# A conformer-style layer on one core: who issues the transfers of the token mixer

## The chip, the cores and the metric

The kernel runs on one core of a Trainium2 chip. A core has TensorE (PE, matrix products into PSUM), VectorE (DVE), ScalarE (ACT), GpSimd (POOL) and SyncE (SP), each with its own queue of instructions that it takes in order, and 16 DMA engines that move data between DRAM and the on-chip SBUF. A transfer is an instruction in the queue of the engine that issues it. The metric is the device time of one execution in microseconds (us); less is better.

## The reference: what is computed

One trunk layer over 1152 tokens (128 of context, 1024 latents) of width 1024:

```python
x = x + HALF_STEP * m[2] * rms_norm(swiglu(h, p['ffn1_w13'], p['ffn1_w2']), gn[1])
h = modulate(rms_norm(x, gn[2]), m[3], m[4])
out, s_fin = token_mixer(h, s0, p, latent)
x = x + m[5] * rms_norm(out, gn[3])
h = modulate(rms_norm(x, gn[4]), m[6], m[7])
x = x + HALF_STEP * m[8] * rms_norm(swiglu(h, p['ffn2_w13'], p['ffn2_w2']), gn[5])
```

The token mixer is what the change touches. It projects h by w_in into r, k, v, g (512 wide each), the three inputs of a short convolution, and two gates of 1024. An RWKV-7 scan runs over r, k, v in both directions, 8 heads of 64:

```python
sa = jnp.einsum('bhij,bhj->bhi', S, -kk_t)
S = (S * w_t[:, :, None, :] + sa[..., None] * (kk_t * a_t)[:, :, None, :]
     + v_t[..., None] * k_t[:, :, None, :])
return S, jnp.einsum('bhij,bhj->bhi', S, r_t)
```

Its outputs are normalised by head, get a bonus (the sum of r k r_k over a head, times v), are gated by sigmoid(g) and projected; the convolution's branch is projected too; the two are merged by the sigmoid gates and projected by w_out.

## The kernel before

Activations lie by channels: tiles of 128 channels by 384 tokens (TW), the tokens in three thirds. Every dense product is made of three products of split operands (lo*hi, hi*lo, hi*hi). `load_w` brings weights in pieces of 128x4x128 (256 KB) into `wst`, of which there are three buffers; ACT makes the high half `whi` (L138), another engine the low half `wlo` (L139), in the mixer POOL.

The mixer lies between the two FFNs and mixes two kinds of work. **Dense products** come from `proj`: 1056 blocks of three matmuls `pj` (L705 to L707) of 128x384; after eight blocks a PSUM bank is full and is evacuated by a function that `proj` is given:

- `to_dram` (L716, L717): ACT copies or passes it through a function into `fso`, and the tile is stored to DRAM: r into rows of `opd`, v into `vd`, the gates into `gd`, `gad`, `gbd`.
- `k_to_dram` (L729, L730): the same for k, stored by `mirrored`, a pattern whose outer dimension is the two heads of a pair (2x64x384).
- `ev_cb` (L797 to L799): POOL multiplies by the convolution, and the tile goes to `cbvd`.

**The scan** has 18 items, a group of heads and a part of the tokens of both directions each. Its operands go through DRAM, since they come by channels and are wanted in other orders. `stage_k` loads r, k and factors (`or` L945, `ok` L890, `od` L892, `oi` L893, v L900), makes kk (stored at L922) and the bonus (ACT L907, stored into `bvd` at L908). `stage_v` loads v (`lv`) and turns it on PE (`vt`). `stage_b`, once for each direction of an item, loads 768 KB of operands (`ops`, L957, one buffer), takes decays (L961 to L982), makes products `scr` (L988), masks them into `e` (ACT L990, POOL L991), and copies the small blocks N out (`nt_`, ACT L995), which L996 stores to `nd`. `solve` loads them back (`un`), inverts them on VectorE (L1036, L1037) with a second trip through DRAM (`xdd`, `tb`), and `step` (L1112 on) does the scan's chunks with `sq`, `yp` and the state tiles `zv`.

A scheduler orders each engine's instructions by priorities and by data. The scan is traced at a high one (`chain()`, `beside()`), `fill(GI)` deals 40 dense blocks after each item, further jobs come in three lanes beside them, and weight loads are moved ahead by `lead`. All DMAs of the mixer stand in SP's queue. PE's order is fixed by the program, so where a scan product is late, the dense blocks behind it wait too.

Of the kernel before, what the change touches and what calls it, by code (L numbers as in the profile page):

```python
# [16 lines left out]
PSUM = bass.MemoryType.PSUM  # L17
DRAM = bass.MemoryType.DRAM
# [8 lines left out]
TW = T // NT  # L27
# [33 lines left out]
def body(ctx: ExitStack, tc: tile.TileContext, I: dict, y_prompt, y_sample, new_state):  # L61
# [16 lines left out]
    def pd(name="pd"):  # L78
        """a PSUM bank for a dense product, in the phases without the scan"""
        rr[0] += 1  # L80
        tag = ("mm", "sq", "yy", "mm", "sq", "oc")[rr[0] % 6]
        return psp.tile([128, TW], F32, name=name, tag=tag, bufs=1 if tag in ("yy", "oc") else 2)
# [5 lines left out]
    # ---------------------------------------------------------------- constants  # L88
# [27 lines left out]
    # ---------------------------------------------------------------- DRAM scratch  # L116
    xd = [[dram.tile([128, TW], F32, name=f"xd{k}_{t}") for t in range(NT)] for k in range(8)]
    # per two pairs: of direction 0 decay and the factors of kk and k, r, kk and k (each the other way round for the
    # second head of a pair), of direction 1 the factors and decay
# [16 lines left out]
    # ---------------------------------------------------------------- pieces  # L136
# [6 lines left out]
    def load_w(src, nk, eng=V):  # L143
        out = []
        with tc.high_priority(offset=lead[0]):
            for k0 in range(0, nk, 4):
                n = min(4, nk - k0)
                st = wp["st"].tile([128, 4, 128], F32, name="wst", tag="wst")
                hi = wp["hi"].tile([128, 4, 128], F32R, name="whi", tag="whi")
                lo = wp["lo"].tile([128, 4, 128], F32R, name="wlo", tag="wlo")  # L150
                SP.dma_start(st[:, :n], src[k0 * 128:(k0 + n) * 128].rearrange("(k p) m -> p k m", p=128))
                split(hi[:, :n], lo[:, :n], st[:, :n], eng)
                out += [(hi[:, k], lo[:, k]) for k in range(n)]
        return out
# [4 lines left out]
    class Beside:  # L159
        """small products, issued after the dense products traced so far"""  # L160
# [14 lines left out]
    class Later:  # L175
        """work beside the dense products, each piece of it so many of them after the one before"""
# [98 lines left out]
    def postnorm(t, O, ssum, gp, spill, want_sum, xpool, sp):  # L275
        """x += gate * rms(O), in place of O; with want_sum the scale of the next norm."""
        G1, G2, G3, GO = GAPS[t == 2 and len(GAPS) > 1]
        xo = []
        for k in range(8):
            x = xpool(k, t)  # L280
            SP.dma_start(x, xd[k][t])
            xo.append(x)
        yield G1
        rs = compact(ssum, 3, ones, 1, 1.0 / D, 1e-6, PE=PB)
        yield G2
        bc = bcast(rs, sp, PB)
        for k in range(8):
            if GO and k:
                yield GO
            a = tmp("poa")  # L290
            for lo, hi, c in SEGS[t]:
                V.scalar_tensor_tensor(out=a[:, lo:hi], in0=O[k][t][:, lo:hi], scalar=gp[:, k, c:c + 1], in1=bc[:, lo:hi], op0=ALU.mult, op1=ALU.mult)
            (V if want_sum or k % 2 else G).tensor_tensor(out=O[k][t], in0=a, in1=xo[k], op=ALU.add)
            if spill:
                SP.dma_start(xd[k][t], O[k][t])
            if want_sum:
                sq_acc(ssum, O[k][t], k == 0, eng=V if k > 5 else G)
        if want_sum:
            yield G3
            rs = compact(ssum, 3, ones, 1, 1.0 / D, 1e-6, PE=PB)  # L300
            yield G2
            return bcast(rs, sp, PB)

    # modulation columns
    def mod_first(mp, h):
        """half of the channels of the first shift and scale, the scale in part on the vector engine"""
# [72 lines left out]
    # ---------------------------------------------------------------- FFN  # L379
# [68 lines left out]
    # ================================================================ FFN 1  # L448
    with ExitStack() as ph:
# [4 lines left out]
        def x_third(t, xp, PE, gap):  # L454
            """a third of the tokens by channels, and the scale of its norm"""
# [123 lines left out]
    # ================================================================ token mixer  # L579
# [3 lines left out]
    # ================================================================ FFN 2  # L583
    with ExitStack() as ph:
# [7 lines left out]
        def rows_of(name, tag, src, k, eng):  # L592
            """a channel block of the last third by tokens"""
            ps = psp.tile([128, 3, 128], F32, name="pfl", tag="sc")
            for i in range(3):
                PB.transpose(ps[:, i], src[:, i * 128:(i + 1) * 128], ident)
            dst = hp.tile([128, 3, 128], F32, name=name, tag=f"{tag}{k}_0")
            if eng is S:
                S.activation(out=dst, in_=ps, func=AF.Copy)
            else:  # L600
                V.tensor_copy(dst, ps)
            return dst
# [50 lines left out]
def mixer(nc, tc, pool, env):  # L653
# [14 lines left out]
    # derived per-channel parameters  # L668
# [9 lines left out]
    # per half of the partitions: the factors of b~ and k~ in the order of its rows  # L678
# [19 lines left out]
    # ------------------------------------------------------------ dense fillers  # L698
    def proj(col, evac, ts=range(NT)):
        """a projection, one block of its rows at a time"""  # L700
        w = load_w(w_in[:, col:col + 128], 8, G)
        for t in ts:
            ps = e.psp.tile([128, TW], F32, name="pj", tag="mm")
            for k, ((hi, lo), (xh, xl)) in enumerate(zip(w, hx(t))):
                PE.matmul(ps, lo, xh, start=(k == 0), stop=False)  # L705
                PE.matmul(ps, hi, xl, start=False, stop=False)  # L706
                ins = PE.matmul(ps, hi, xh, start=False, stop=(k == 7))  # L707
                if k < 7:
                    yield ins
            evac(t, ps)  # L710
            yield ins

    def to_dram(dst, func=AF.Copy, **kw):
        def f(t, ps):
            o = e.tmp("fso", tag="s")
            S.activation(out=o, in_=ps, func=func, **kw)  # L716
            SP.dma_start(dst[:, t * TW:(t + 1) * TW], o)  # L717
        return f

    def mirrored(p, row, sign, t0, n):  # L720
        """a row of the operands of a pair, and for the second head the row after or before it"""
# [4 lines left out]
    def k_to_dram(p):  # L726
        def f(t, ps):
            o = e.tmp("fso", tag="s")
            S.activation(out=o, in_=ps, func=AF.Copy)  # L729
            SP.dma_start(mirrored(p, 5, -1, t * TW, TW), o)  # L730
# [15 lines left out]
    with ExitStack() as ph:  # L746
# [26 lines left out]
        def job_conv(j):  # L773
# [21 lines left out]
            def ev_cb(t, ps):  # L795
# [3 lines left out]
                SP.dma_start(cbvd[j][:, t * TW:(t + 1) * TW], o)  # L799
# [68 lines left out]
        def shifted(t, d):  # L868
            """(column, source token, count) of the tokens of a third that have a neighbour."""
# [12 lines left out]
        # ------------------------------------------------------------ per pair, per block of tokens  # L882
        def stage_k(p, t0, n, bon=True):
            """kk and the bonus, of a pair of heads and a block of tokens"""
# [17 lines left out]
            def bonus():  # L902
# [5 lines left out]
                SP.dma_start(bvd[p][:, t0:t0 + n], o)  # L908
# [18 lines left out]
        def stage_v(p, t0, n, zv):  # L927
            """V by tokens, of a pair of heads and a block of tokens"""
# [19 lines left out]
        def zi(g, b):  # L948
            """the place of V and of the outputs of a quarter of the latents"""
            return b if g == 0 else (1, 0, 3, 2)[b]  # L950

        def stage_b(g, d, t0, A, it):
            """operands of a direction for the two chunks of tokens t0.., of two pairs of heads"""
# [42 lines left out]
            SP.dma_start(diag(nd[it], d, s0, nb), N)  # L996
# [11 lines left out]
        def diag(t_, d, s0, nb):  # L1008
            """the blocks of a direction, partition by partition of the rows of a chunk"""
            return bass.AP(tensor=t_.tensor, offset=t_.offset + (d * 16 + s0 * 4) * 1024, ap=[[32, 128], [4096, nb], [1, 32]])  # L1010

        def every4(t_, r, n):
            """the partitions 4 v + r of a tile, first n columns"""
# [3 lines left out]
        def solve(A, it):  # L1017
            """(I - N)^-1 of the 32 diagonal 32x32 blocks of an item.

            Partition 4 v + rep has block v: the inverses of its four 8x8 diagonal blocks, and  # L1020
            of the whole the columns 8 b + 2 rep + cc, which follow from them row block by row block."""
# [69 lines left out]
        def group(products):  # L1091
            """products issued in a row, the first of which has the operand that comes last"""
# [8 lines left out]
        def cells(w, s):  # L1101
            """the states of two pairs in the operands of a chunk, head by head"""
# [9 lines left out]
        def step(A, chains, first):  # L1112
            """one chunk of two pairs of heads in each direction: (chunk of the item, its operands w[:, s], decay,
            outputs, next state). State and V are in w[:, s], a block of columns for each head: the state on
            the head's own half of the partitions, V on the other."""
# [185 lines left out]
        # the jobs that become possible after an item's scan  # L1301
# [3 lines left out]
        class Lane:  # L1305
            """jobs beside the scan: one at a time, a piece of it every so many blocks of dense products"""
# [28 lines left out]
        def fill(n):  # L1335
            """blocks of dense products, and the products beside the scan that are due"""
# [55 lines left out]
    # ================================================================ merge, output projection  # L1392
# [82 lines left out]
```

## Time and profile before

| | |
|---|---|
| median of 3 runs | 3303.96 us (3299.4 to 3308.2) |
| profiled execution, span | 3303.1 us; no other time is given for it |
| PE / PE weight loads busy | 3036.7 / 2850.3 us |
| VectorE / ACT / POOL busy | 1914.0 / 1201.1 / 395.3 us |
| mixer, roughly | 909 to 2215 us of the span |
| DMA | 347.25 MB, mean 105 GB/s |

The span is that of one execution under the hardware profiler. Instructions that issue a DMA don't count as busy. A piece "SPq" of the chain is time in which the chain's transfer was being issued in SP's queue, and "DMA" its time from then on until it landed.

### The profile page before, as it was taken

The page shows a single profiled execution, that of the slowest core. Times are in us where ns is not written, and L with a number is a line of the kernel's source. Part 1 is how long each engine was busy: PE and PEld are TensorE (multiplying, and loading weights), DVE is VectorE, ACT ScalarE, POOL GpSimd, SP SyncE. Part 2 cuts the span into 40 slices and gives each one's busy share as a digit, 9 for nine tenths or more (in the row PEclk, how much of TensorE's full clock was granted, in tenths as well). Part 3 has the DMA queues.
Part 4 walks back from the last instruction along what each step waited for, and adds up shares of the span by engine and source line. Part 5 has one row for each costly group of instructions (what it writes and reads, how often), then busy time and mean ns, then how long its engine had stood idle before and what let it go on. Part 6 is the DMA issues. An engine that isn't in the chain of part 4 may idle for free.

```text
span 3303.1 us, 54285 instructions
## 1 busy us (share of the span) xinstructions
PE 3036.7 (92%) x20956; PEld 2850.3 (86%) x20956; DVE 1914.0 (58%) x4282; ACT 1201.1 (36%) x2726; POOL 395.3 (12%) x327
## 2 busy tenths in 40 slices
PE   8999999999989677788888889899989999999998
PEld 5999999999978566677767777779989999999998
DVE  7535665556962244577877778856683233323356
ACT  5521111114546133355535456432454211121244
POOL 1000000001240111122323122100120000000012
PEclk9999999999999788799988899999999999999999
DMA  8423333225445242323333333345632111111244
GB/s 268 144 63 94 96 110 90 83 78 164 151 116 190 80 121 72 111 84 106 99 88 102 108 106 105 103 124 155 190 109 87 38 45 40 45 40 41 83 144 131
DMA packets 521742, 347.25 MB, mean 105 GB/s; under 512 B 76096, under 2 KB 497292, under 8 KB 521484
## 3 DMA queue, kind: packets, MB, share of 16 engines
q1 hardware_dynamic: 520856, 343.31, 35.2%
q8 instruction: 164, 2.69, 0.3%
q14 instruction: 94, 0.77, 0.1%
q10 hardware_dynamic: 308, 0.44, 0.0%
q0 software_dynamic: 320, 0.04, 0.0%
HBM read 277.37 MB, written 66.32 MB: 104 GB/s over the span
## 4 chain that ended last, share of the span: by engine, by line
PE 67%; DVE 16%; DMA 10%; ACT 3%; issue 2%; SPq 1%; POOL 0%; DVEq 0%; ACTq 0%; POOLq 0%
PE po L211 6%; PE po L210 6%; PE po L212 6%; PE pg L211 5%; PE pg L212 5%; PE pg L210 5%; PE pu L211 5%; PE pu L210 5%; PE pu L212 5%; PE pj L705 3%; PE pj L707 3%; PE pj L706 3%; DMA ops<-opd 3%; DMA oi<-opd 2%; DVE un L1036 1%
## 5 line engine op out<-in xcount | busy, mean ns | idle before, releaser
L138 ACT ACTIVATE whi<-wst 128x512 fp32r<-128x512 f32 (+1 forms) x578 | 353.1, 612 | 792.7 <-PE po L212 389.4
L139 DVE TENSOR_TENSOR wlo<-wst,whi 128x512 fp32r<-128x512 f32 (+1 forms) x480 | 325.2, 678 | 305.8 <-ACT whi L138 296.2
L705 PE MATMUL pj<-hh,wlo 128*128 128x384 f32 x1056 | 393.8, 373 | 4.3 <-ACT xcs L783 1.8
L706 PE MATMUL pj<-hl,whi 128*128 128x384 f32 x1056 | 393.7, 373 | 2.3 <-DVE hl L265 1.3
L707 PE MATMUL pj<-hh,whi 128*128 128x384 f32 x1056 | 391.9, 371 | 0.0
L211 PE MATMUL pg<-hl,whi 128*128 128x384 f32 x1056 | 355.9, 337 | 6.4 <-POOL hl L263 5.0
L210 PE MATMUL po<-ah,wlo 128*128 128x384 f32 x1056 | 355.4, 337 | 3.0 <-ACT ah L138 3.0
L210 PE MATMUL pg<-hh,wlo 128*128 128x384 f32 x1056 | 356.8, 338 | 1.4 <-DVE wlo L139 1.3
L211 PE MATMUL po<-al,whi 128*128 128x384 f32 x1056 | 354.8, 336 | 0.4 <-DVE al L139 0.4
L212 PE MATMUL pg<-hh,whi 128*128 128x384 f32 x1056 | 355.0, 336 | 0.0
L210 PE MATMUL pu<-hh,wlo 128*128 128x384 f32 x1056 | 355.0, 336 | 0.0
L212 PE MATMUL po<-ah,whi 128*128 128x384 f32 x1056 | 354.2, 336 | 0.0
L211 PE MATMUL pu<-hl,whi 128*128 128x384 f32 x1056 | 353.8, 335 | 0.0
L212 PE MATMUL pu<-hh,whi 128*128 128x384 f32 x1056 | 353.5, 335 | 0.0
L273 POOL TENSOR_TENSOR ss<-ss,sqt 128x384 f32<-128x384 f32 x78 | 88.5, 1138 | 1679.5 <-ACT sqt L272 1675.0
L426 DVE TENSOR_TENSOR sil<-sil,pu 128x384 f32<-128x384 f32 x132 | 72.8, 552 | 353.0 <-PE pu L212 353.0
L398 DVE TENSOR_TENSOR o<-o,po 128x384 f32<-128x384 f32 x288 | 159.2, 553 | 168.2 <-PE po L212 167.5
L705 PEld LDWEIGHTS pj<-hh,wlo 128*128 128x128 f32 x1056 | 215.6, 204 | 13.8 <-issue 2.1
L706 PEld LDWEIGHTS pj<-hl,whi 128*128 128x128 f32 x1056 | 215.9, 204 | 10.8 <-DVE hl L265 2.2
L707 PEld LDWEIGHTS pj<-hh,whi 128*128 128x128 f32 x1056 | 215.7, 204 | 7.0
L139 POOL TENSOR_TENSOR wlo<-wst,whi 128x512 fp32r<-128x512 f32 x98 | 134.6, 1376 | 622.7 <-ACT whi L138 486.1
L211 PEld LDWEIGHTS pg<-hl,whi 128*128 128x128 f32 x1056 | 199.7, 189 | 8.8 <-POOL hl L263 6.5
(621 smaller groups left out, 5848.6 us busy)
## 6 DMA issues: line engine op xcount, KB each, us to landing
wst<-in_ffn_w SPq DMA_DIRECT2D x324, 256.0 KB
wmod<-in_w_mod SPq DMA_DIRECT2D x144, 256.0 KB
ops<-opd SPq DMA_DIRECT2D x36, 768.0 KB
wst<-in_w_in SPq DMA_DIRECT2D x94, 256.0 KB
wst<-in_ffn_w SPq DMA_DIRECT2D x96, 192.0 KB
xo<-xd SPq DMA_DIRECT2D x64, 192.0 KB
wst<-in_w_out SPq DMA_DIRECT2D x48, 256.0 KB
opd<-zv SPq DMA_DIRECT2D x24, 384.0 KB
```

Source lines behind the costliest of these rows:

```text
L138: S.activation(out=hi, in_=src, func=AF.Copy)
L139: eng.tensor_tensor(out=lo, in0=src, in1=hi.bitcast(F32), op=ALU.subtract)
L210: PE.matmul(ps, lo, xh, start=(k == 0), stop=False)
L211: PE.matmul(ps, hi, xl, start=False, stop=False)
L212: later.tick(PE.matmul(ps, hi, xh, start=False, stop=(k == nk - 1)))
L273: eng.tensor_tensor(out=ssum, in0=ssum, in1=q, op=ALU.add)
L398: V.tensor_tensor(out=O[m][t], in0=O[m][t], in1=ps, op=ALU.add)
L426: V.tensor_tensor(out=s, in0=s, in1=pu, op=ALU.mult)
L705: PE.matmul(ps, lo, xh, start=(k == 0), stop=False)
L706: PE.matmul(ps, hi, xl, start=False, stop=False)
L707: ins = PE.matmul(ps, hi, xh, start=False, stop=(k == 7))
L1036: V.tensor_tensor(out=pv, in0=a, in1=b, op=ALU.mult)
```

## The change

The weight loads of `proj` are issued by POOL, the engine that makes `wlo` out of them. The stores of `to_dram`, `k_to_dram`, the bonus and N are issued by ACT, which makes these tiles, and the store of `ev_cb` by POOL, which makes that one. Sizes, patterns and buffers stay. The rest of the diff takes comments and docstrings out and leaves line numbers as they were.

```diff
-    def load_w(src, nk, eng=V):
+    def load_w(src, nk, eng=V, queue=SP):
...
-                SP.dma_start(st[:, :n], src[k0 * 128:(k0 + n) * 128].rearrange("(k p) m -> p k m", p=128))
+                queue.dma_start(st[:, :n], src[k0 * 128:(k0 + n) * 128].rearrange("(k p) m -> p k m", p=128))
...
     def proj(col, evac, ts=range(NT)):
-        w = load_w(w_in[:, col:col + 128], 8, G)
+        w = load_w(w_in[:, col:col + 128], 8, G, G)
...
             S.activation(out=o, in_=ps, func=func, **kw)
-            SP.dma_start(dst[:, t * TW:(t + 1) * TW], o)
+            S.dma_start(dst[:, t * TW:(t + 1) * TW], o)
...
             S.activation(out=o, in_=ps, func=AF.Copy)
-            SP.dma_start(mirrored(p, 5, -1, t * TW, TW), o)
+            S.dma_start(mirrored(p, 5, -1, t * TW, TW), o)
...
                 G.tensor_tensor(out=o, in0=o, in1=u_[t], op=ALU.mult)
-                SP.dma_start(cbvd[j][:, t * TW:(t + 1) * TW], o)
+                G.dma_start(cbvd[j][:, t * TW:(t + 1) * TW], o)
...
                 S.activation(out=o, in_=o, func=AF.Identity, bias=gb4[:, p:p + 1])
-                SP.dma_start(bvd[p][:, t0:t0 + n], o)
+                S.dma_start(bvd[p][:, t0:t0 + n], o)
...
-            SP.dma_start(diag(nd[it], d, s0, nb), N)
+            S.dma_start(diag(nd[it], d, s0, nb), N)
```

In the program this moves 94 weight loads (L151) and 12 stores (L799) to POOL, and 152 stores (84 at L717, 12 at L730, 20 at L908, 36 at L996) to ACT. The scheduler places everything anew.

SP's queue early in the mixer, while the first operands of the scan are loaded; the rows that stood there before and don't any more have a minus:

```order
 L922 DMA opd_110<-oi 2x64x256
 L890 DMA ok<-opd_110 128x1x256
 L892 DMA od<-opd_110 128x1x256
-L151 DMA wst<-in_w_in 128x4x128
 L957 DMA ops<-opd_110 128x12x128
 L893 DMA oi<-opd_110 128x1x256
-L730 DMA opd_110<-fso 2x64x384
-L717 DMA vd_113<-fso 128x384
 L900 DMA or<-vd_113 128x256
```

Ahead of the operand load L957 the weight load is gone, and ahead of the load of v (L900) the two stores.

ACT's queue in the same part of the program, from the decays of the first item to the store of its first N, before the change. In brackets stands what an instruction waits for: the work of an engine, or (DMAHW, DMASW) one of the counters that finished transfers raise, of which the transfers issued by SP and ACT share eight:

```order
L716 ACTIVATE fso<-pj 128x384 [waits PE_49]
L138 ACTIVATE whi<-wst 128x512 [waits DMAHW0_49,PE_49,Pool_49]
L907 ACTIVATE or<-or,gb_9063 128x256 [waits DVE_49]
L990 ACTIVATE e_10899<-scr 64x4x128 [waits DVE_49]
L995 ACTIVATE nt__10933<-ab_10895 32x128 x2
L990 ACTIVATE e_10899<-scr 64x4x128 [waits DVE_49]
L995 ACTIVATE nt__10933<-ab_10895 32x128 x2
L1000 ACTIVATE ab_10895<-bkt 128x512 [waits PE_49]
```

And in the changed program:

```order
L907 ACTIVATE or<-or,gb_9063 128x256 [waits DVE_49]
L138 ACTIVATE whi<-wst 128x512 [waits DMASW6_49,PE_49,Pool_49]
L908 DMA bvd_117<-or 128x256 [waits Activation_49]
L716 ACTIVATE fso<-pj 128x384
L717 DMA vd_113<-fso 128x384 [waits DMAHW0_49,Activation_49]
L990 ACTIVATE e_10899<-scr 64x4x128 [waits DVE_49]
L995 ACTIVATE nt__10933<-ab_10895 32x128 x2
L990 ACTIVATE e_10899<-scr 64x4x128 [waits DVE_49]
L995 ACTIVATE nt__10933<-ab_10895 32x128 x2
L1000 ACTIVATE ab_10895<-bkt 128x512 [waits PE_49]
L996 DMA nd_9071<-nt__10933 128x4x32 [waits DMAHW2_49,Activation_49]
```

Three stores now stand between the copies, each waits for the copy that makes its tile ("Activation"), and two of them for a counter besides.

POOL's queue around the masks of the first item in the changed program; before, the same rows stood there without the L151:

```order
+L991 TENSOR_TENSOR e_10899<-e_10899,cst 64x4x128 x2
+L139 TENSOR_TENSOR wlo<-wst,whi 128x512
+L151 DMA wst<-in_w_in 128x4x128
+L139 TENSOR_TENSOR wlo<-wst,whi 128x512
+L151 DMA wst<-in_w_in 128x4x128
+L139 TENSOR_TENSOR wlo<-wst,whi 128x512
+L151 DMA wst<-in_w_in 128x4x128
+L991 TENSOR_TENSOR e_10900<-e_10900,cst 64x4x128 x2
```

Each weight load follows the instruction that frees its buffer, in the same queue.

## Rows read from the trace of the kernel before

**Rows 1.** The page's busy times of each engine, and the share of each in the chain of work that ended last.

```profile
PE 3036.7 (92%) x20956; PEld 2850.3 (86%) x20956; DVE 1914.0 (58%) x4282; ACT 1201.1 (36%) x2726; POOL 395.3 (12%) x327
...
PE 67%; DVE 16%; DMA 10%; ACT 3%; issue 2%; SPq 1%; POOL 0%; DVEq 0%; ACTq 0%; POOLq 0%
```

**Rows 2.** Busy time by stretch of the span, for three parts of the mixer: start and end, length, each engine's busy us with its instructions, the granted TensorE clock, the busy share of the DMA engines, GB/s.

```profile
909.00:1060.00 151.00, 133.69 (x702) 124.73 (x700) 75.17 (x134) 80.23 (x150) 36.99 (x31) 0.94 0.45 145
1060.00:1340.00 280.00, 199.31 (x1454) 177.11 (x1453) 114.18 (x298) 86.35 (x217) 39.24 (x30) 0.79 0.35 103
1340.00:2215.00 875.00, 762.77 (x7686) 646.60 (x7685) 661.56 (x1828) 420.59 (x1140) 192.82 (x145) 0.92 0.35 99
```

**Rows 3.** The chain of work that ended last, pieces of it in order of time between 1060 and 1340 us: start, length, what.

```profile
1073.78 7.54 DMA opd<-fso
...
1097.42 3.97 SPq L151
...
1107.48 1.51 SPq L730
1109.10 9.07 DMA vd<-fso
1118.19 2.14 DMA or<-vd
...
1132.62 3.38 SPq L717
1136.11 9.09 DMA oi<-opd
...
1156.68 3.20 SPq L908
...
1249.74 10.69 DMA bvd<-or
...
1295.61 0.65 SPq L908
...
1318.62 1.42 SPq L908
```

**Rows 4.** SP's queue in order of time just after 1100 us: start, length of the issuing instruction, line, transfer.

```profile
1101.44 1.34 SPq L957 DMA_DIRECT2D ops<-opd  x1
1102.83 4.56 SPq L893 DMA_DIRECT2D oi<-opd  x1
```

**Rows 5.** The timeline of ACT and of PE at the same place: start, length, instruction, and in brackets how long the engine had been idle and what ended it.

```profile
1111.02 0.42 ACT L961 ACTIVATE sg<-ops 128x256 f32<-128x256 f32 x1 [11.05 <-DMA ops<-opd]
1116.77 3.48 PE L988 MATMUL scr<-e,bk 64*128 64x128 f32 x16 [10.09 <-DVE bk L978]
1123.96 0.60 ACT L1000 ACTIVATE ab<-bkt 128x512 f32<-128x512 f32 x1
```

**Rows 6.** What SP's queue waited for: us in total, times, longest. The first row is for the whole mixer (909 to 2215 us), the others for 1060 to 1340.

```profile
SPq L717 <- ACT fso L716: 75.2, 28, 10.7
...
SPq L151 <- POOL wlo L139: 32.0, 12, 10.3
...
SPq L996 <- ACT nt__11901 L995: 14.0, 1, 14.0
SPq L717 <- ACT fso L716: 9.8, 5, 4.2
```

**Rows 7.** The chain again, at 1593 us.

```profile
1593.21 2.90 DMA wst<-in_w_in
```

**Rows 8.** Durations of the issuing instructions in SP's queue by line (ns, least/median/most, first and last start in us). L996 has a row for each of its tiles; the first of its 36 is shown.

```profile
L717 SPq DMA_DIRECT2D gad<-fso x24: 319/326/1068, 1820.3 to 2200.3; - x24
L717 SPq DMA_DIRECT2D gbd<-fso x23: 319/332/506, 1854.8 to 2209.9; - x23
L717 SPq DMA_DIRECT2D opd<-fso x12: 319/439/3987, 918.7 to 1244.0; - x12
L717 SPq DMA_DIRECT2D vd<-fso x12: 319/440/2076, 946.7 to 1327.9; - x12
L717 SPq DMA_DIRECT2D gd<-fso x12: 319/434/860, 1332.7 to 1542.1; - x12
...
L730 SPq DMA_DIRECT2D opd<-fso x12: 492/516/1512, 931.7 to 1284.5; - x12
...
L908 SPq DMA_DIRECT2D bvd<-or x20: 315/358/4068, 1054.1 to 2003.5; - x20
...
L996 SPq DMA_DIRECT2D nd<-nt__10933 x1: 371/371/371, 1123.9 to 1123.9; - x1
```

**Rows 9.** Issues by ACT and by POOL at the start of the program: of ACT's four the longest and the shortest (start, length), of POOL's ten one of 4 rows and the one of 32 (ns, least/median/most).

```profile
0.74 0.59 ACTq L509 DMA_DIRECT2D rows<-in_c_ctx  x1
1.37 0.33 ACTq L512 DMA_DIRECT2D rows<-in_norm_g  x1
...
L528 POOL DMA_DIRECT2D rows<-in_k_k x1: 518/518/518, 2.5 to 2.5; - x1
...
L528 POOL DMA_DIRECT2D rows<-in_mu_shift x1: 535/535/535, 6.1 to 6.1; - x1
```

**Rows 10.** The dense products L705 over the whole program: count and mean (ns) of one matmul, and of PE's idle time before them what POOL's low halves account for (us, times).

```profile
L705 PE MATMUL pj<-hh,wlo 128*128 128x384 f32 x1056 | 393.8, 373 | 4.3 <-ACT xcs L783 1.8
...
  POOL wlo L139: 0.3, 1
```

## The prediction

> **What bounds the kernel now.** I read the busy line first [rows 1]: TensorE (PE) works 3036.7 of 3303.1 us, so all that any reordering can win is the 266 us in which it stands. The windows say where it stands [rows 2]: in the mixer, 909 to 2215 us, it is idle 17 + 81 + 112 = 210 us, and the worst stretch is 1060 to 1340, where PE has 199 of 280 us and the granted clock is 0.79. In the same stretch ScalarE (ACT) is busy 86 us and GpSimd (POOL) 39, so neither is short of time there. The chain that ended last, cut to this stretch, shows what is late instead [rows 3]: single transfers of 7 to 11 us, and pieces of SP's queue ("SPq") that last 1.4 to 4 us although they only issue. The queue's own timeline explains those pieces [rows 3, 4]: an issue that usually takes under half a microsecond [rows 8] took 3.97 us at 1097.42 and 4.56 at 1102.83, one behind the other, and the operand load L957 between them left SP only at 1101.44. Its tile arrived when ACT and VectorE woke at 1111.02, and PE stood 10.09 us before its products L988 [rows 5]. So in this stretch the scan waits for loads that wait in SP's line. SP itself also stands still for others' sake [rows 6]: 32.0 us for a weight buffer (L151), 14.0 us for one tile N (L996), 9.8 us for evacuated tiles (L717). While it stands, every load behind is late. From 1340 on the chain runs through loads that stay on SP (ops, oi) and through VectorE; the moved kinds hold one notable piece there, a weight load of 2.90 us [rows 7].
>
> **The change, part by part.** *Taken off SP.* 94 weight loads, 84 + 12 + 20 + 36 = 152 stores that ACT now issues, and 12 that POOL issues.
>
> (a) The moved issues on the chain: 3.97 + 1.51 + 3.38 + 3.20 + 0.65 + 1.42 = 14.1 us [rows 3]. These can no longer hold SP. I take all of it; the least is nothing, if the loads behind are then held just as long by each other, as L893 was with 4.56 us [rows 4].
>
> (b) Landings of moved stores on the chain: bvd 10.69 and vd 9.07 us. A load of 128 KB out of the same vd, right behind one of them, took 2.14 us [rows 3]; so 6.9 + 8.6 = 15.5 us are delay by what stood ahead in the queue, or by the sixteen DMA engines. Half of it is taken, 7.7 us, since the trace does not say which. The bounds are 0 and all three landings with opd<-fso, 27.3 us.
>
> (c) The weight load at 1593: 2.9 us [rows 7], from 0 to 2.9, taken whole.
>
> Gain: 14.1 + 7.7 + 2.9 = 24.7 us, with 0 and 14.1 + 27.3 + 2.9 = 44.3 us as its ends.
>
> *Added to ACT.* (d) By the median issue times on SP [rows 8]: 24 x 0.326 + 24 x 0.332 + 12 x (0.439 + 0.440 + 0.434) for L717, 12 x 0.516 for L730, 20 x 0.358 for L908, 36 x 0.370 for L996, together 58 us. ACT's only issues in the trace, four at the start, took 0.33 to 0.59 us [rows 9], so 152 of them lie between 50 and 90 us, and SP's medians stand for them. ACT's busy time in the mixer rises from 80 + 86 + 421 = 587 to 645 of 1306 us. What of it reaches the end: ACT holds 3% of the chain, about 99 us, of its 1201 us of work [rows 1]; that is 8%, and 17% if all of these 99 lay in the mixer's 587. 58 us make 5 to 10.
>
> (e) Its waits. A store stands behind the instruction that makes its tile and waits for the end of it, and in the changed program 110 of the 152 also wait for a transfer that last used the same completion counter. That transfer stands 24 to 245 PE instructions earlier; at 280 us for 1454 instructions [rows 2] these are 5 to 47 us, so only those near the lower end can still be under way, next to landings of up to 10.7 us. One in eight, 14 of 110, with 3 us each is 42 us. Queued behind such a store are evacuations of dense products, weight halves (whi) and the scan's copies (e, nt, oi), and PE waits for these. Together (d) and (e) are 100 us, 8 to 17 us on the path; I take 12. The ends are 0 and, if all 110 wait 3 us, 17% of 388, 66 us. One tile is moved behind more: N's store now follows the copy L1000, 0.60 us [rows 5], which for the last N of 18 items would be at most 11 us; SP's own delay of the same store (14.0 and more) covers it, so it counts nothing.
>
> *Added to POOL.* (f) 106 issues. POOL's only transfers in the trace take 0.52 us for 4 rows and 0.54 for 32 [rows 9]; carried on at that slope, 512 rows come to 0.8 us, so 55 to 85 us in all. POOL has 269 of the mixer's 1306 us busy [rows 2], so it goes to a quarter. The cover: weights were never late, PE waited 0.3 us for wlo in all 1056 blocks [rows 10], and the loads are placed far ahead. Behind a load stand the tiles e (L991, 72 of them), which the scan does need; with a load in issue 6% of the time and half of 0.8 us left, 72 of them lose 2 us. I count 0; the ends are 0 and +15, if the first five loads of the mixer, which have the least lead, each hold PE up for the 2.90 us that one took on the chain [rows 7].
>
> Here the Trainium skill speaks against the change: "SBUF — State Buffer", the box on the "DVE blocks DMA" trap, says that a transfer issued from GpSimd has its descriptors written by GpSimd, which is locked out while VectorE runs certain copies. By its figures, 620 ns alone and 3100 beside such a copy, 94 loads would cost POOL up to 290 us, an estimate from that page; no run here shows it yet.
>
> (g) *Order.* In the changed program the scan's last chunk stands ahead of dense block 985 of 1056, before it ahead of 1001. So 16 x 3 x 0.373 us = 18 us [rows 10] of dense work that filled waits of the scan come after it. If the scan needed them, up to +18; I count 0, since the waits they would fill are the ones that (a) shortens.
>
> **Sum.** The profiled span is 3303.1 us, 0.9 under the median 3303.96, which I take as what lies around it. 3304.0 - 24.7 + 12 = **3291 us**, a gain of 0.4%. Some 10 us, 0.3%, is what a measurement of this kernel can tell from no change.
>
> **Rivals.**
>
> *No change that can be measured.* The transfers and their bytes are the same, and the DMA share of the stretch is 0.35 already [rows 2]. If the late landings are the sixteen engines' doing, (b) is nothing and half of (a) comes back as other loads' waiting: 3304 - 7 - 3 + 12, 3306 us. For it speaks that L893's oi, which stays on SP, was as slow as what moves (9.09 us) [rows 3]. Against it: SP's standing for L151 and L996 [rows 6] is no engine's doing. The Trainium skill has this as a rule, "DMA: Bandwidth & Descriptors", section "Issuing engines are not separate DMA queues": all issuers share the same 16 DMA engines, and several of them save only the time of issuing.
>
> *Slower, by ACT.* Each store is now a wait in the queue that empties PSUM for PE and makes the scan's operands. If half of the 110 stores wait 3 us, ACT has 58 + 165 = 223 us more, at 17% 38 on the path: 3304 - 25 + 38 = 3317 us; if all do, 66, and 3345. It decides from 145 us of ACT on, that is 29 waits of 3 us. For it: on SP the same stores stood long (L717 75.2 us in 28 waits over the mixer [rows 6]), and in 1340 to 2215 ACT is busy 421 of 875 us, so its line is rarely empty. Against it: those SP waits were for the tile itself, which on ACT is just made.
>
> *Slower or level, by late weights.* With (f) at its end, +15, and (g) at half, +9: 3291 + 24 = 3315, or 3306 with the one alone. For it: POOL must finish issuing before its next wlo or e can start. Against it: the 0.3 us of [rows 10], a lead that a microsecond per load does not use up.
>
> *A larger gain.* All of (a) to (c), 44.3 us, and ACT's issues at the 5 us of (d): 3304 - 44 + 5 = 3265 us. For it: shorter waits in SP also make the unmoved loads earlier, and PE stands 81 us in that stretch.
>
> **Chances.** The forecast 32%, the larger gain 14%; no change 20%; slower by ACT 26%; late weights 8%, half of it within 10 us. So faster 0.46, same 0.20 + 0.04 = 0.24, slower 0.26 + 0.04 = 0.30. Of the slower cases the far half and of the gains the farthest few are left out: 3258 to 3335. The forecast's own range, with ACT's 8 and 17 and (b) at 0 or whole, is 3279 to 3304.
>
> **What would show it.** If (a) holds, SP's issues over 3 us become few between 1060 and 1340, PE's wait of 10 us before L988 shrinks and the stretch's granted clock rises over 0.79. If (b) holds, vd and bvd land in 2 to 4 us. For (d) and (e): rows of stores on ACT with some 0.35 us each, ACT near 645 us plus short waits; if PE's waits for fso, oi and whi grow and ACT's queue waits for transfers, the slower rival is right. For (f): POOL's rows of L151 under 1 us and PE's wait for wlo still near nothing; rows of 3 us would refute it. For (g): the waits in 1340 to 2215 grow beyond 112 us. The forecast is wrong above all if ACT's stores wait for counters more often than one time in eight.

## The result, and the profile after

The changed kernel takes 3335.34 us (median of 4 runs, 3334.37 to 3337.33), the kernel before 3302.34 beside it: 1.0102 of it, 95% interval 1.0078 to 1.0127. It is 33 us slower where 13 us less were forecast. The sign is that of the rival "slower, by ACT", but the runs below price ACT's part at some 4 of the 33 us.

The page of the changed kernel: busy times, shares of the chain, and the DMA queues (packets, MB, share of 16 engines' span).

```profile
PE 3042.4 (91%) x20956; PEld 2864.2 (86%) x20956; DVE 1919.0 (58%) x4282; ACT 1200.2 (36%) x2726; POOL 466.2 (14%) x433
...
q1 hardware_dynamic: 433952, 292.70, 29.5%
q0 software_dynamic: 8608, 27.05, 2.8%
q10 hardware_dynamic: 35852, 24.04, 2.4%
...
PE 66%; DVE 15%; DMA 12%; issue 3%; ACT 2%; SPq 1%; POOL 0%; DVEq 0%; ACTq 0%; POOLq 0%
```

Against [rows 1], ACT works as long as before, VectorE 5 us and PE 6 us longer, POOL 71 us longer: 106 instructions more, its issues, which this page counts as busy, unlike those of SP and ACT. Of 347 MB, 24 now go by ACT's queue (q10) and 27 by POOL's (q0). DMA's share of the chain went from 10 to 12%, ACT's fell from 3 to 2.

The same three stretches as in [rows 2], in the same columns:

```profile
909.00:1060.00 151.00, 129.69 (x661) 122.05 (x660) 77.80 (x131) 73.43 (x136) 46.21 (x47) 0.91 0.42 136
1060.00:1340.00 280.00, 190.71 (x1392) 169.47 (x1391) 104.41 (x283) 85.89 (x209) 48.57 (x44) 0.80 0.32 96
1340.00:2215.00 875.00, 749.20 (x7612) 636.85 (x7611) 664.40 (x1798) 419.08 (x1144) 243.21 (x217) 0.90 0.35 99
```

PE does 4 + 9 + 14 us less in them. The stretch from 1060 to 1340, where the gain was expected, is worse than before, and the mixer ends at 2248 us instead of 2213. After it little changed (1086 us to the end, 1090 before).

The chain in that stretch, some of its pieces, as in [rows 3]:

```profile
1106.29 7.54 DMA opd<-oi
1114.30 14.28 DMA oi<-opd
...
1142.51 6.36 DMA opd<-oi
1148.93 9.82 DMA oi<-opd
...
1167.31 9.96 DMA opd<-oi
...
1310.22 8.74 DMA bvd<-or
```

The moved issues (SPq L151, L717, L730, L908) are gone from it. In their place stand transfers of the scan itself, of those that stay on SP: kk's store (opd<-oi, L922) and the load of the factors (oi<-opd, L893), which took 14.28 us at 1114.30. SP's queue at that place, columns as in [rows 4]:

```profile
1106.29 0.52 SPq L922 DMA_DIRECT2D opd<-oi  x1
1106.91 0.50 SPq L890 DMA_DIRECT2D ok<-opd  x1
1107.50 2.24 SPq L892 DMA_DIRECT2D od<-opd  x1
1113.89 0.36 SPq L957 DMA_DIRECT2D ops<-opd  x1
1114.30 7.49 SPq L893 DMA_DIRECT2D oi<-opd  x1
```

A piece "DMA" of the chain begins where its issue begins, at 1114.30 in both views: the 14.28 us hold the 7.49 of issuing. A piece "SPq" is the issue that stood ahead of the next piece's transfer in the queue. With nothing of the fillers left in the line, the issue of L893 took 7.49 us (4.56 before, [rows 4]). I counted all issues over 3 us that start between 1060 and 1340 in the traces, with their lines:

| kernel | SP's issues there | over 3 us | together | lines |
|---|---|---|---|---|
| before | 139 | 6 | 24.0 us | L151, L893, L717, L908 three times |
| after | 81 | 5 | 25.3 us | L893, L1023, L945 twice, L892 |
| e1 (queues only, below) | 83 | 8 | 38.4 us | L892 twice, L893, L945 three times, L1055, L1047 |
| e8 (halves, below) | 216 | 0 | 0 | |

Before, five of the six long issues fell on filler transfers (L151, L717) or on the bonus store (L908) that happened to stand behind the mirrored transfers (2x64xn). With these gone, the scan's own loads stand there and take the wait.

What the moved issues cost where they are now, columns as in [rows 8]; the last row is the only time that PE waited for POOL's low halves before L705, as in [rows 10]:

```profile
L717 ACTq DMA_DIRECT2D vd<-fso x12: 321/327/352, 950.6 to 1359.4; - x12
...
L730 ACTq DMA_DIRECT2D opd<-fso x12: 490/502/604, 934.8 to 1307.6; - x12
...
L908 ACTq DMA_DIRECT2D bvd<-or x20: 321/326/390, 1063.6 to 2019.0; - x20
...
L151 POOL DMA_DIRECT2D wst<-in_w_in x93: 747/767/1092, 905.3 to 2201.0; - x93
...
  POOL wlo L139: 0.4, 1
```

On ACT the longest of the 152 issues takes 1.34 us, where SP's took up to 4; on POOL the median load takes 0.77 us, near the 0.8 of (f).

### The profile page after: what moved, and what is told of

Its sections match the earlier page's. It is cut to its first block, busy times and chain, and to the rows that moved or that the text cites. A ratio compares the mean times of both kernels' runs of the same rounds, so it can differ in the third digit from the quotient of the medians.

```text
span 3333.8 us, 54258 instructions
## 1 busy us (share of the span) xinstructions
PE 3042.4 (91%) x20956; PEld 2864.2 (86%) x20956; DVE 1919.0 (58%) x4282; ACT 1200.2 (36%) x2726; POOL 466.2 (14%) x433
## 4 chain that ended last, share of the span: by engine, by line
PE 66%; DVE 15%; DMA 12%; issue 3%; ACT 2%; SPq 1%; POOL 0%; DVEq 0%; ACTq 0%; POOLq 0%
PE po L211 6%; PE po L210 6%; PE po L212 6%; PE pg L211 5%; PE pg L212 5%; PE pg L210 5%; PE pu L211 5%; PE pu L212 5%; PE pu L210 5%; DMA oi<-opd 3%; DMA opd<-oi 3%; PE pj L705 3%; PE pj L706 3%; PE pj L707 3%; DMA ops<-opd 3%
## 5 line engine op out<-in xcount | busy, mean ns | idle before, releaser
L705 PE MATMUL pj<-hh,wlo 128*128 128x384 f32 x1056 | 397.2, 376 | 3.4 <-ACT fso L716 1.7
L705 PEld LDWEIGHTS pj<-hh,wlo 128*128 128x128 f32 x1056 | 217.4, 206 | 12.7 <-issue 3.3
```

## The experiments

A kernel's moved transfers also make the scheduler place everything anew, so the change is two things: other queues, and another order. The first two kernels separate them. An order can be held by adding an edge without a wait between each pair of neighbours on an engine, taken from the other kernel's program. In the traces of the kernels held in the old order (e1, e5 to e10) the mixer's 9826 PE instructions stand as before, but for 12 to 36 places, and e7 and e10 below, held in this way, take as long as the kernel before. All ratios are to runs of the kernel before beside them.

### e1: the new queues in the old order

The edit, shortened:

```diff
 (the changed kernel, and after the body)
+for e, at in ORDER_OF_BEFORE.items():      # PE, ACT, DVE, POOL computing, and what is left on SP
+    for x, y in zip(at, at[1:]):
+        tc.add_manual_dep(l[y], l[x].name, NoSync)
```

> The changed kernel's issuing engines (94 weight loads on POOL, 152 stores on ACT, 12 on POOL), but PE, VectorE, ACT's and POOL's computing instructions and what is left on SP are held in the order of the kernel before. Theory ORDER (the loss comes from the scheduler's new order, which puts the scan's products ahead of dense blocks that used to fill its waits): the loss is gone and part (a) and (b) of the prediction shows, 3285 to 3303 us. Theory QUEUES (the loss comes from ACT standing at its stores, or from transfers that land later): as slow as the changed kernel, 3325 to 3345 us, with PE waiting for ACT's results.

Measured: 1.0091 (1.0077 to 1.0104), 30 us slower. The theory that only the order loses falls: in an unchanged order of all computing, the new queues alone lose. SP's queue in this kernel at the place of [rows 4], and PE at that of [rows 5]:

```profile
1100.20 6.28 SPq L892 DMA_DIRECT2D od<-opd  x1
1109.71 0.36 SPq L957 DMA_DIRECT2D ops<-opd  x1
1110.12 4.46 SPq L893 DMA_DIRECT2D oi<-opd  x1
```

```profile
1124.26 2.07 PE L988 MATMUL scr<-e,bk 64*128 64x128 f32 x9 [14.11 <-DVE bk L978]
```

The row ahead of L957 used to be the weight load with its 3.97 us; now it is od's load with 6.28, and L957 leaves SP 8.3 us later than before (at 1109.71, not 1101.44; 3.5 of these us had been lost ahead of this place, as L922's issue shows, 1098.84 against 1095.37). PE stands 14.11 us, not 10.09. Since the order is the same, each transfer can be set against itself, issue to landing, mean over the 20 of a kind in the mixer: the moved bvd went from 4.78 to 3.62 us, but on SP or<-opd from 3.27 to 4.36, od from 7.41 to 8.26, kk's store from 6.75 to 7.47. What the moved stores gained, the scan's transfers lost. The time lost doesn't follow these landings, though, as e5 and e7 show below.

### e2: the old queues in the new order

The kernel before with edges that hold the changed kernel's order; all transfers on SP.

> The counterpart: all transfers on SP as before, but every engine's computing instructions, and the transfers that the change leaves on SP, held in the changed kernel's order. Theory ORDER: slow without any moved transfer, 3325 us or more, since SP also has to do what that order supposes it is rid of. Theory QUEUES: about as before, 3295 to 3310 us.

Measured: 1.0048 (1.0035 to 1.0060), 16 us slower. The order alone loses too, about half of what the queues do; the two together give 1.0102 and do not add up. Busy times of the mixer, from its first dense product to its last (columns as in [rows 2]), of before, after, e1 and e2 in this order:

```profile
909.00:2213.00 1304.00, 1093.77 (x9826) 946.44 (x9825) 849.01 (x2255) 585.45 (x1502) 269.05 (x205) 0.89 0.36 105
```

```profile
909.00:2248.00 1339.00, 1101.73 (x9842) 958.87 (x9841) 861.00 (x2265) 589.63 (x1512) 340.56 (x310) 0.88 0.35 104
```

```profile
909.00:2254.00 1345.00, 1115.73 (x9830) 967.34 (x9829) 857.78 (x2257) 588.52 (x1506) 343.80 (x308) 0.88 0.35 102
```

```profile
909.00:2244.00 1335.00, 1099.38 (x9823) 956.09 (x9822) 848.10 (x2262) 587.55 (x1507) 267.26 (x204) 0.88 0.36 104
```

Length less PE's busy time is idle: 210, 237, 229 and 236 us. In the new order the loss is mostly standing (+27, +25); in the old order with new queues it is standing (+19) and slower products (+22).

Where PE stands in the new order, two of its waits in the changed kernel (in all, times, longest):

```profile
PE scr L988 <- DVE e L982: 34.7, 11, 9.9
PE trx L1064 <- DMA tb<-xdd: 27.4, 4, 12.6
```

and in the kernel before:

```profile
PE trx L1064 <- DMA tb<-xdd: 4.8, 1, 4.8
...
PE scr L988 <- DVE e L982: 6.3, 6, 1.9
```

They go with the order: in e2, with the old queues, they are 30.5 and 16.5 us, in e1, with the new queues in the old order, 7.1 and 7.9. Other waits shrink, so that 25 to 27 us more are left in all. That these products now stand too few dense blocks behind what they wait for, as (g) feared, fits, but was not shown.

### e3 and e4: each half, placed anew

e3 has only the loads of `proj` on POOL; e4 only the stores on ACT and POOL.

> Only the 94 weight loads go to POOL, the stores stay on SP; the scheduler places everything anew. Theory ORDER: any sign, -15 to +30 us around 3303, by how much dense work the new order leaves behind the scan. Theory QUEUES (ACT's stores): 3290 to 3305 us, since ACT has nothing new; if POOL's issues were at fault instead, 3320 us or more.

> Only the stores move (152 to ACT, 12 to POOL), the weight loads stay on SP; the scheduler places everything anew. Theory QUEUES (ACT's stores): most of the loss, 3320 to 3340 us. Theory ORDER: any sign again, and the time follows the scan's place among the dense blocks and not ACT's own waits.

Measured: 1.0058 (1.0044 to 1.0071) and 1.0080 (1.0066 to 1.0094). Each half loses, each with an order of its own, so these two don't tell queue from order. The next three do.

### e5, e6, e7: each part in the old order

> Only the 94 weight loads on POOL, with all computing and the rest of SP's queue held in the order of the kernel before. Theory LINE (SP's single line kept the fillers' transfers behind the scan's; on queues of their own they start earlier, run beside the scan's loads and make these land later, as the run with only the issuing engines changed shows: or 3.27 to 4.36 us, od 7.41 to 8.26, the load of un further behind): slower, +5 to +20 us. Theory ACT (ACT's copies are held up by its stores): no change, within 6 us of before, since ACT does nothing new.

> Only the 96 evacuation stores L717 and L730 on ACT, the rest held as before. LINE: slower by +5 to +20 us, with the scan's loads landing later while vd, opd and gd land earlier. ACT: slower by about two thirds of the whole loss of 30 us, +15 to +25, with PE waiting longer for fso, e, oi from ACT.

> Only the 56 stores of the scan's own tiles, bonus L908 and N L996, on ACT, the rest held as before. LINE: these are the scan's own and not filler traffic, so no loss, -10 to +5 us. ACT: about a third of the loss, +8 to +15 us, since they stand among the scan's copies.

| moved, order held | ratio to before | us |
|---|---|---|
| e5: 94 weight loads, to POOL | 1.0079 (1.0065 to 1.0093) | +26 |
| e6: 96 evacuation stores, to ACT | 1.0015 (1.0004 to 1.0026) | +5 |
| e7: 56 stores of bonus and N, to ACT | 0.9997 (0.9984 to 1.0010) | -1 |

The theory ACT falls: 96 stores in its queue cost about 5 us (1 to 9 by the interval), 56 nothing, and the large loss is in the kernel where ACT has nothing new. The three add up to the 30 us of e1. The loss of the queues is the weight loads, which I had priced at nothing, and it is larger than the 5 to 20 us that I expected under LINE.

How a delay of 2 us becomes more is seen at one place. In the kernel before, SP's queue:

```profile
1891.48 0.50 SPq L893 DMA_DIRECT2D oi<-opd  x1
1892.08 0.42 SPq L151 DMA_DIRECT2D wst<-in_w_in  x1
```

In e5, SP's and POOL's:

```profile
1898.70 0.50 SPq L893 DMA_DIRECT2D oi<-opd  x1
...
1898.61 0.79 POOL L151 DMA_DIRECT2D wst<-in_w_in  x1 [0.29 <-POOL wlo L139]
```

The weight load went out behind the scan's load before, and beside it in e5. PE's wait there, and the 20 us that follow it, first of before, then of e5:

```profile
1898.89 0.49 PE L168 MATMUL bon<-od,cst 128*128 128x128 f32 x2 [3.05 <-DVE od L898]
...
1898.90:1918.90 20.00, 19.41 (x186) 16.28 (x186) 16.43 (x46) 9.10 (x28) 2.57 (x2) 0.91 0.29 83
```

```profile
1907.96 0.80 PE L168 MATMUL bon<-od,cst 128*128 128x128 f32 x2 [4.98 <-DVE od L898]
...
1908.00:1928.00 20.00, 20.00 (x125) 16.64 (x126) 12.08 (x33) 4.99 (x16) 0.76 (x1) 0.50 0.28 80
```

oi took 5.9 us from issue to landing and not 4.0, PE stood 4.98 us and not 3.05, and the granted clock of the next 20 us is 0.50, not 0.91: after the longer stand the products run at the lower of the two levels (1.2 GHz), 125 of them in the time of 186. Over the whole mixer e5 has 12 us more standing and 20 us more PE time for the same products (1336 us with 1114 busy, by the same view as above). So in this execution most of the loss is the clock's; that waits a little longer set it off is seen at this place and argued for the rest.

What makes these waits longer is open. A general slowing of the scan's loads isn't seen: from issue to landing, mean over the mixer, or takes 3.10 us in e5 (3.27 before), oi 6.51 (6.38), od 7.65 (7.41), ops 6.11 (6.05), while e7, which loses nothing, has or at 4.18 and od at 7.73. The loss also comes late: up to the dense products at 1896 us e5 is 7 us behind, at the last one 32.

### e9 and e10: is it POOL?

e9 issues the 94 loads from ACT instead; e10 leaves them on SP and gives POOL seven small fills behind each low half, 1.2 us from first to last where a load's issue takes 0.77, both in the old order. e10's kernel differs in one more place: each step of the modulation at the start takes seven buffers, not two. Its mixer starts at 909 us, like that of before.

> As the run with the weight loads alone moved, all else held in the order of before, but the 94 loads are issued by ACT, not POOL. Moving them to POOL cost 28 us. Theory LINE (the loads leave SP's line and run beside the scan's loads, whatever queue they have instead): slow again, +12 to +30 us. Theory POOL (its issuing time of 0.79 us each, or the way its queue is served, is at fault): within 8 us of before.

> The kernel before, held in its own order, all transfers on SP, with seven small fills of an unused tile on POOL behind each of its 94 low halves: they stand where POOL's weight loads stood and take about their time (0.7 us). The fills are extra work and change no result. Theory POOL, by time on that engine: slow, +10 to +28 us. Theory LINE, or one of the way POOL's queue is served: within 6 us of before.

Measured: e9 1.0035 (1.0019 to 1.0052), 12 us; e10 0.9993 (0.9979 to 1.0007). POOL's time costs nothing. On ACT's queue the loads cost 12 us (6 to 17 by the interval), at the lower edge of what theory LINE expected; on POOL's queue they cost 14 more. The standing in the profiled executions of e5 and e9 is alike (222 and 226 us, though that of e9 was 12 us over its median); they differ in PE's busy time (1114 and 1102 us), that is by the clock. These are single executions: that of e10 has 10 us more PE time than before and 8 less standing. Why the loads lose more by POOL's queue is open. One difference is seen in the page: POOL's queue moved 24.7 MB in 7,840 packets in e5, ACT's 25.1 MB in 49,940 in e9, so a packet is six times as large; whether that is the reason was not tried.

### e8 and e11: the transfers that make the line long

The rows of SP's queue point to the mirrored transfers, whose outer dimension is the two heads. In the mixers of before, the changed kernel and e1, all 23 issues on SP over 3 us began while one to three mirrored transfers were still under way; 1270 issues began with none under way, and none of these took over 3 us. The trace also sets them apart: the completion counter of a mirrored transfer has 3 updates, that of the scan's other transfers and of a half 16.

```diff
-        return bass.AP(..., offset=base, ap=[[64 * ps + 2 * sign * T, 2], [ps, 64], [1, n]])
+        return [bass.AP(..., offset=base + h * (64 * ps + 2 * sign * T), ap=[[ps, 64], [1, n]]) for h in range(2)]
...
-            SP.dma_start(k, mirrored(p, 5, -1, t0, n))
+            [SP.dma_start(k[64 * h:64 * h + 64], m) for h, m in enumerate(mirrored(p, 5, -1, t0, n))]
```

and likewise at L730, L892, L893 and L922. e8 keeps the old order of computing (SP's own queue isn't held: 38 of its 1109 places from 900 us on are taken anew, a pair of halves counted as one, none more than five off); e11 lets the scheduler place everything anew.

> The kernel before, all on SP and computing in its order, but each mirrored transfer (2x64xn: L730, L890, L892, L893, L922) is issued as two of 64 rows. It tests what makes SP's line long: if it is these transfers, whose two-row outer dimension spreads them badly over the DMA engines (6 to 8 us landing), they land in 2 to 4 us, SP's issues over 3 us go, and the kernel gains 15 to 50 us although SP issues 92 more. If the line is long for its number of transfers alone, the halves land as late and nothing is gained, 0 to +20 us.

> The kernel before with each mirrored transfer (2x64xn) issued as two of 64 rows, all on SP, and the scheduler free to place everything anew. In the old order this gained 126 us. Expected 3165 to 3215 us: the order costs or gives some 20 us either way.

Measured: 0.9625 (0.9608 to 0.9642), and 0.9573 (0.9560 to 0.9585), 3165.64 us: 142 us less than before, and faster than both kernels of the case. e8's 126 us are far above the 15 to 50 expected. PE's longest group of waits between 1060 and 1340 before, then in e8 the landing of oi's halves over the whole program, the same group, and that stretch:

```profile
PE cps L168 <- ACT oi L896: 34.2, 4, 12.0
```

```profile
DMA to landing us min/median/max: 2.2/2.9/4.6
...
PE cps L168 <- ACT oi L896: 8.5, 4, 4.8
...
1060.00:1340.00 280.00, 243.84 (x2013) 214.29 (x2012) 167.19 (x435) 116.64 (x297) 52.13 (x40) 0.93 0.43 122
```

Where oi stood on the chain with 9.09 us [rows 3] and took 6.3 at the median, it now lands in 2.9; SP issues 216 transfers in the stretch and none takes over 3 us; PE works 244 of 280 us, not 199, at a granted clock of 0.93. The line was long by these few transfers, not by the number of what stands in it: SP issues 92 more.

### e12 to e15: the change with halves

e12 is the changed kernel with halves, placed anew. e13 and e14 are e8 with only the loads on POOL, and only the stores moved, in e8's order; e15 is e14 placed anew.

> The changed kernel (94 loads on POOL, 152 stores on ACT, 12 on POOL) with the mirrored transfers issued as halves, placed anew by the scheduler. If the change only lost because the scan's loads are slow two-row transfers that suffer from neighbours, moving transfers off SP now costs nothing or gains: within 10 us of the kernel with halves alone, or below it. If it loses for any traffic that leaves SP's line, it stays 15 to 35 us above.

> The kernel with the mirrored transfers as halves in the old order (3183.5 us, 0.9625 of before), with the 94 weight loads on POOL, all computing and the rest of SP's line held. If the loads' loss of 28 us needs the slow two-row transfers to collide with, it shrinks to under 10 us: ratio to before 0.960 to 0.966. If it comes from any load that leaves SP's line, 12 to 30 us: 0.966 to 0.972.

> The same kernel with halves in the old order, with the 164 stores moved (ACT and POOL's 12) and the weight loads left on SP, the rest held. The stores cost 5 us or nothing in the old order before; if that holds, ratio to before 0.960 to 0.966, 0.9625 being the kernel without the move. ACT's issues grow to 164 by the halves of L730; if ACT's time were the matter, 0.968 or more.

> Halves, the 164 stores on ACT and POOL, weight loads on SP, placed anew by the scheduler. In the held order the stores gained 9 us with halves; if that is worth more than the draw of a new order, it comes in below the kernel with halves alone placed anew (0.9573 of before): 0.950 to 0.957. If a new order costs more than that, as it did before the halves (stores placed anew 1.0080, held about 1.001), 0.958 to 0.968.

| halves, with | order | ratio to before |
|---|---|---|
| nothing moved (e8) | old | 0.9625 (0.9608 to 0.9642) |
| loads on POOL (e13) | old | 0.9667 (0.9646 to 0.9688) |
| stores on ACT, 12 on POOL (e14) | old | 0.9598 (0.9580 to 0.9616) |
| nothing moved (e11) | anew | 0.9573 (0.9560 to 0.9585) |
| stores (e15) | anew | 0.9599 (0.9577 to 0.9622) |
| both (e12) | anew | 0.9653 (0.9634 to 0.9673) |

The loads on POOL lose 0.42% (14 us) even without two-row transfers, about half of the 26 us with them: so about half of their loss seems to need the slow transfers as neighbours, as far as the intervals tell. The stores, which cost 5 us before, now gain about 9 (the intervals of e8 and e14 just overlap); placed anew they are 9 above e11, again with overlapping intervals. The whole change still loses some 26 us (e12 against e11).

## Why the prediction was wrong

Split by what moves, the forecast was -7 us for the weight loads (L151's piece of (a), (c), (f)), -6 for the stores (the rest of (a), (b), (d), (e)) and 0 for the order (g). Measured one by one they are +26 (e5), +4 (e6, e7) and +16 (e2), together +33. The steps that failed are (f) and (g), both put at nothing, and the gain (a).

**What bounds the kernel** was read rightly in one half: the stretch from 1060 to 1340 does wait for loads in SP's line, and a cure of the line (e8) was worth 126 us: the mixer took 1184 us with 1055 busy, 81 us less standing and 39 us less time for the same products. The other half was wrong: I took the long issues for something that leaves SP with the transfer being issued. They are the wait of the next transfer, whichever it is, behind the mirrored ones.

**(a), 14.1 us "taken whole": failed.** Without it the sum would have been 3305, no change. After the change 25.3 us of long issues stand in the stretch, before 24.0, now all on the scan's loads. The lower bound that I gave ("if the loads behind are then held just as long by each other, as L893 was") is what happened; the row with 4.56 us on a scan load [rows 4] was the sign that I saw and did not weigh.

**(b), 7.7 us: the mechanism held for the moved stores and was paid for by others.** bvd landed in 3.62 us at the mean in e1, not 4.78; or, od and kk's store took 1.09, 0.85 and 0.72 us longer. By the rule "Issuing engines are not separate DMA queues" of the Trainium skill ("DMA: Bandwidth & Descriptors") all issuers share the same DMA engines, and several of them save only the time of issuing. The traces agree, in that what some transfers gained in e1 others lost.

**(c)** can't be seen by itself: in e5 the weight loads off SP lost 26 us in all.

**(d) and (e), 12 us on ACT: too high.** ACT's issues took 0.33 and 0.50 us at the median, as counted, but the 152 stores in the old order cost about 5 - 1 = 4 us, with whatever they gain on SP in it (e6, e7). The rival "slower, by ACT" had the sign, by luck.

**(f), 0 us with an end of +15: mis-sized, 26 us.** Its parts were right: 0.77 us an issue, weights never late (0.4 us), no cost by POOL's time (e10). The longest issue of a load was 1.09 us. The Trainium skill ("SBUF — State Buffer", section "A bandwidth-pool intuition that's wrong (but worth ruling out)") has a transfer issued by GpSimd take about 3100 ns beside a VectorE copy where it takes about 620 alone; POOL's issues show no such wait in this kernel. What I had no term for is that the weight loads lose by leaving SP's queue: 12 us on ACT's (e9), 26 on POOL's (e5), by longer waits of PE and the lower clock behind them. Which transfer or engine makes the waits longer stays open.

**(g), 0 us with an end of +18: mis-sized, 16 us.** e2 has this order with the old queues and loses 0.48%. I argued that the waits which the 16 dense blocks used to fill would get shorter by (a); (a) failed, and the waits for e L982 and tb grew from 11 to 62 us in the changed kernel, to 47 in e2. The sign named for it came: PE's standing from 1340 to 2215 grew from 112 to 126 us.

What stays open: why the weight loads lose by leaving SP's queue, why 14 us more on POOL's than on ACT's, and why the two losses (e1 and e2) together are hardly more than the larger.

## What to carry to other kernels

A long issue in a queue belongs to what stands ahead of it, so look up the shapes of the two or three transfers before it, and cure those, before moving what happens to wait. A queue of its own isn't free for filler traffic, even where the issuing engine has time to spare: here it cost the weight loads 12 us on one engine and 26 on the other. Where a scheduler decides the order, hold the old order to price the move itself, and price the new order with nothing moved.

## What the runs showed that I had not expected

A load of 128 KB with an outer dimension of two takes 6.4 to 7.4 us from issue to landing, at the mean (ok, od, oi before), a half of 64 rows 2.6 to 3.0 (e8), and splitting them, with 92 issues more on SP, was worth 126 to 142 us of 3300. A wait of PE that grew by 2 us, in a mixer of 1300, came with a lower granted clock for the 20 us behind it (0.50 against 0.91), and in e5 the products' own time grew by 20 us where the standing grew by 12.
